# A weight-stationary product whose half block runs its 512-column products over all four banks before its 256-column ones

## The chip, the cores and the metric

The kernel runs on one core of one Trainium2 chip. The metric is the device time of one execution in microseconds (us). Five engines work side by side, each through its own queue of instructions: PE (TensorE, the matmuls; its weight loads are shown apart as PEld), DVE (VectorE), ACT (ScalarE), POOL (GpSimd) and SP (SyncE), which here only issues transfers. Matmuls write to eight banks of PSUM.

## The reference

A two-layer decoder trunk on 256 tokens of width 2048 in float32. Layer 0 mixes with eight stick-breaking attention heads and eight gated-linear-attention heads, layer 1 with a Mamba-2 state-space mixer (here "the second mixer"). After each mixer come a squared-ReLU MLP and a gated input embedding; a final RMSNorm ends it. Cut to what matters:

```python
def squared_relu_mlp(x, w_up, w_down):                 # 2048 -> 8192 -> 2048
    return jnp.square(jax.nn.relu(x @ w_up)) @ w_down

def ssd_mixer(x, w_in, ...):
    z, xbc, dt = jnp.split(x @ w_in, ...)              # 2048 -> 4096 + 6144 + 64
    ...                                                # conv, chunked scan, norm
    return (y * silu(z)) @ w_out

def reference(x, p, ...):
    h = x
    for i in range(2):
        hn = rms_norm(h, norm_mix[i])
        h = h + (sb_gla_mixer(hn, ...) if i == 0 else ssd_mixer(hn, ...))
        h = h + squared_relu_mlp(rms_norm(h, norm_mlp[i]), w_up[i], w_down[i])
        h = h + jax.nn.sigmoid(h @ ple_w_gate[i]) * (p[i] @ ple_w_proj[i])
    return rms_norm(h, final_norm)
```

Nearly all of the arithmetic lies in the products of `h` with the large weight matrices.

## The kernel before

Each operand of a large product is split in two, a rounded high part and the rest as a low part, and three of the four partial products are kept: high by high, high by low, low by high. Activations lie in memory as `[x_hi | x_lo]`, 256 columns each. Weights arrive by DMA in blocks of 1 MB (`load_block`, tile `wraw`, three buffers) and are split in half blocks of 128 x 1024 by `split_weights`: ACT casts the high part (L92, tile `whi`), DVE subtracts it for the low part (L93, tile `wlo`). Each of `whi` and `wlo` has three buffers.

`feature_major` computes the products whose output has features on partitions: the input projections of both mixers and the `up` half of each MLP. It works in groups of 512 output features, that is four PSUM banks (tiles `acc0` to `acc3`) of 128 features by 512 columns. The pool `acc_ps` holds five such banks, so that a new group finds one bank free, and gets the others when the old group's have been read. A group takes four weight blocks, each of two half blocks: eight half blocks per group. A half block holds eight stationary tiles of 128 x 128, two for each bank. With weights stationary, a bank gets from them two products of 512 columns (`whi` against `[x_hi | x_lo]`, L132) and two of 256 columns (`wlo` against `x_hi`, L137). There are 60 such groups, 480 half blocks, and 3840 products of either kind: 8 groups in the first mixer (numbers 0 to 7 in what follows), 16 in the four `up` quarters of the first MLP (8 to 23), 20 in the second mixer (24 to 43), 16 in the second MLP (44 to 59).

When a group's four banks are full they are read by the evacuation. In the MLP (`up`, L430 on) it calls `add_halves` for each bank: ACT copies the right half out (L197, tile `right`, three buffers), DVE adds the left half to it (L198). Then one DVE instruction squares (L434), and the result is split again. In the second mixer the evacuation of the `z` columns is L803 on ACT and L804 on DVE. Between its groups the second mixer also runs steps of its scan. The ones spoken of later: transposes of `xs` on PE (L721), their product with `dt` on DVE (L722, tile `xdt`), a product on POOL (L727, tile `xdd`), and a matmul of `xdd` on PE (L736, tile `st_ps`).

The other large products (`quad_major`, L371 to L373; `token_major`, L186 to L188) keep activations stationary and stream the weights; the change does not touch them.

The order in which the source issues instructions is not the order on an engine: a scheduler, with costs of its own, places the instructions of the whole program into the queues. Within a queue an instruction that waits holds up those behind it.

Of the kernel before, what the change touches and what calls it, by code (L numbers as in the profile page):

```python
# [26 lines left out]
def hybrid_trunk(  # L27
# [60 lines left out]
    def split_weights(src_raw, cols, pool=None):  # L88
        pool = pool or wts
        hi = pool.tile([P, cols], F32R, tag="whi", name="whi", padded_shape=[P, 1024])  # L90
        lo = pool.tile([P, cols], F32R, tag="wlo", name="wlo", padded_shape=[P, 1024])
        nc.scalar.copy(out=hi, in_=src_raw)  # L92
        nc.vector.tensor_tensor(out=lo, in0=src_raw, in1=hi.bitcast(F32), op=ALU.subtract)  # L93
        return hi, lo
# [3 lines left out]
    def load_block(src, cols=2048):  # L98
        raw = wts.tile([P, cols], F32, tag="wraw", name="wraw", padded_shape=[P, 2048])
        if halve.pop() if halve else False:  # L100
            nc.sync.dma_start(raw[:, : cols // 2], src[:, : cols // 2])
            nc.sync.dma_start(raw[:, cols // 2 :], src[:, cols // 2 :])
        else:
            nc.sync.dma_start(raw, src)
        return raw
# [10 lines left out]
    def feature_major(blocks, kb_n, xt, evac, width=4, kts=4, evac_group=None):  # L116

        for grp, srcs in enumerate(blocks):
            banks = [acc_ps.tile([P, 512], F32, tag="acc", name=f"acc{n}") for n in range(width)]
            cols = kts * width * P  # L120
            per = 1024 // (width * P)
            if per > kts:
                per = kts
            for kb in range(kb_n):
                raw = load_block(srcs[kb], cols)
                for c0 in range(0, kts, per):
                    hi, lo = split_weights(raw[:, c0 * width * P : (c0 + per) * width * P], per * width * P)
                    for n in range(width):
                        for j in range(per):
                            k = kb * kts + c0 + j  # L130
                            o = (j * width + n) * P
                            nc.tensor.matmul(banks[n], lhsT=hi[:, o : o + P], rhs=xt(k),  # L132
                                             start=(k == 0), stop=False, skip_group_check=True)
                        for j in range(per):
                            k = kb * kts + c0 + j
                            o = (j * width + n) * P
                            nc.tensor.matmul(banks[n][:, T : 2 * T], lhsT=lo[:, o : o + P], rhs=xt(k)[:, 0:T],  # L137
                                             start=False, stop=(k == kb_n * kts - 1), skip_group_check=True)
                yield
            if evac_group is not None:  # L140
                evac_group(grp, banks)
            else:
                for n in range(width):
                    evac(grp * width + n, banks[n])
            yield
# [274 lines left out]
    def mlp(i, x):  # L420
        r2 = []

        with tc.tile_pool(name=f"mlp{i}", bufs=2) as tmp:
# [3 lines left out]
            def up(q):  # L427
                hid[0] = operand(4, f"hid{q}_")

                def evac(grp, banks):  # L430
                    t4 = tmp.tile([P, 4, T], F32, tag="t4", name="t4")
                    for n in range(4):
                        add_halves(t4[:, n, :], banks[n])
                    nc.vector.scalar_tensor_tensor(out=t4, in0=t4, scalar=0.0, in1=t4, op0=ALU.max, op1=ALU.mult)  # L434
                    pg = hid[0](4 * grp, True)
                    nc.scalar.copy(out=pg[:, :, 0:T], in_=t4)
                    nc.vector.tensor_tensor(out=pg[:, :, T : 2 * T], in0=t4, in1=pg[:, :, 0:T].bitcast(F32), op=ALU.subtract)
                    m = 2 * grp + 1
                    if m in SEVEN:
                        a11, a21, a12, a22 = (t4[:, 2 + kk, t * P : (t + 1) * P] for kk in range(2) for t in range(2))  # L440
                        e = ev.tile([P, 4, P], F32, tag="row", name="s4")
                        nc.vector.tensor_tensor(out=e[:, 0, :], in0=a21, in1=a22, op=ALU.add)
                        nc.vector.tensor_tensor(out=e[:, 1, :], in0=e[:, 0, :], in1=a11, op=ALU.subtract)
                        nc.vector.tensor_tensor(out=e[:, 2, :], in0=a11, in1=a21, op=ALU.subtract)
                        nc.vector.tensor_tensor(out=e[:, 3, :], in0=a12, in1=e[:, 1, :], op=ALU.subtract)
                        if grp % 2 == 0:
                            sums["pg"] = page([P, 2, 1024], "ss", F32R)
                        sums[m] = sums["pg"][:, grp % 2, :]
                        ef = e.rearrange("p e t -> p (e t)")
                        nc.scalar.copy(out=sums[m][:, 0:512], in_=ef)  # L450
                        nc.vector.tensor_tensor(out=sums[m][:, 512:1024], in0=ef, in1=sums[m][:, 0:512].bitcast(F32), op=ALU.subtract)

                pace(feature_major(grid(mlp_up[i], range(4 * q, 4 * q + 4), 4), 4, x, None, evac_group=evac), [])
# [153 lines left out]
    def mixer1(xu, raw):  # L607
        with tc.tile_pool(name="mix1", bufs=1) as mid, tc.tile_pool(name="mix1t", bufs=2) as tmp:
# [159 lines left out]
            def fm(nb, evac, xt=x):  # L768
                return feature_major(grid(ssd_in, nb, 4), 4, xt, evac)
# [83 lines left out]
    def mixer0():  # L853
        with tc.tile_pool(name="mix0", bufs=1) as mid, tc.tile_pool(name="mix0t", bufs=2) as tmp:
# [52 lines left out]
            def fm(groups, evac, xt=x):  # L907
                return feature_major(grid(ab_in, groups, 4), 4, xt, evac)
# [269 lines left out]
```

## Time and profile before

| | us |
|---|---|
| median of three runs | 2729.83 (2729.3 to 2730.58) |
| the profiled execution's own time | 2729.36 |
| its span, first to last instruction | 2727.6 |
| PE busy | 2694.5 (99%) |
| DVE busy | 1908.3 (70%) |
| ACT busy | 1418.4 (52%) |
| mean granted TensorE clock | 0.997 |
| DMA, mean | 187 GB/s |

A row of a timeline is: start and duration in us, engine, line and operation, output and inputs, sizes, and how many instructions of that kind follow one another; in square brackets the idle time of the engine just before and what ended it. Matmuls are pipelined: one of 512 columns is shown with about 0.39 us, but the next starts about 0.23 us after it, so the pace is read from starts. A row of windows gives, for a stretch, its length and the busy time and number of instructions of PE, PEld, DVE, ACT and POOL, then clock, DMA share and GB/s.

### The profile page before, as it was taken

How to read it: one execution, taken by the hardware profiler on the slowest of the kernel's cores; microseconds unless marked ns; L12 is line 12 of the kernel's file. 1: busy time of each engine (PE TensorE's matmuls, PEld its weight loads, DVE VectorE, ACT ScalarE, POOL GpSimd, SP SyncE). 2: the span in 40 equal slices, each digit the busy share in tenths (PEclk: the TensorE clock that was granted, in tenths of full speed). 3: DMA queues.
4: the chain of work that ended last, by engine and by line, in shares of the span. 5: the costliest groups of instructions: out<-in, count | busy, mean ns of one | idle time of the engine just before them, and what ended most of it. 6: DMA issues, size and time to landing. Idle time of an engine off the chain costs nothing.

```text
span 2727.6 us, 35652 instructions
## 1 busy us (share of the span) xinstructions
PE 2694.5 (99%) x14004; PEld 2275.1 (83%) x14004; DVE 1908.3 (70%) x2569; ACT 1418.4 (52%) x1933; POOL 174.3 (6%) x258
## 2 busy tenths in 40 slices
PE   7999999999999999999999999999999999999998
PEld 6888878888888888888888888888888888888886
DVE  7455666776867767558988888754677776776755
ACT  6455455545545445556655655644454544545544
POOL 2000000000000000003232122300000000000000
PEclk9999999999999999999999999999999999999999
DMA  6544355555555555554555554455555555555544
GB/s 252 185 155 155 123 185 185 201 188 193 206 186 196 192 191 210 182 185 155 201 195 177 186 198 173 171 187 197 186 201 186 205 196 185 187 199 188 219 176 147
DMA packets 73304, 510.36 MB, mean 187 GB/s; under 512 B 8672, under 2 KB 8864, under 8 KB 12720
## 3 DMA queue, kind: packets, MB, share of 16 engines
q1 hardware_dynamic: 70640, 497.32, 51.3%
q10 hardware_dynamic: 2496, 10.78, 1.1%
q8 instruction: 109, 1.79, 0.3%
q14 instruction: 59, 0.48, 0.0%
HBM read 505.90 MB, written 2.16 MB: 186 GB/s over the span
## 4 chain that ended last, share of the span: by engine, by line
PE 95%; DVE 3%; ACT 1%; issue 1%; POOL 0%; DMA 0%; DVEq 0%; ACTq 0%
PE acc L132 31%; PE acc L137 15%; PE q L371 8%; PE q L373 8%; PE q L372 8%; PE acct L187 7%; PE acct L186 7%; PE acct L188 7%; DVE wlo L93 1%; PE y_ps L745 1%; PE x_tp L280 1%; PE y_ps L747 0%; DVE x L114 0%; DVE a_cv L675 0%; ACT whi L92 0%
## 5 line engine op out<-in xcount | busy, mean ns | idle before, releaser
L93 DVE TENSOR_TENSOR wlo<-wraw,whi 128x1024 fp32r<-128x1024 f32 (+1 forms) x936 | 1131.9, 1216 | 643.6 <-ACT whi L92 638.2
L92 ACT CAST whi<-wraw 128x1024 fp32r<-128x1024 f32 (+1 forms) x936 | 964.7, 1038 | 1007.5 <-PE acc L132 478.1
L132 PE MATMUL acc<-x,whi 128*128 128x512 f32 x3840 | 1213.6, 398 | 9.6 <-ACT whi L92 9.6
L137 PEld LDWEIGHTS acc<-x,wlo 128*128 128x128 f32 x3840 | 716.9, 188 | 175.7 <-DVE wlo L93 9.2
L137 PE MATMUL acc<-x,wlo 128*128 128x256 f32 x3840 | 753.4, 279 | 5.2 <-DVE wlo L93 5.1
L132 PEld LDWEIGHTS acc<-x,whi 128*128 128x128 f32 x3840 | 590.8, 189 | 19.0 <-ACT whi L92 9.8
L371 PE MATMUL q<-whi,hid 128*128 128x512 f32 x884 | 344.7, 390 | 0.0
L373 PE MATMUL q<-whi,hid 128*128 128x512 f32 x884 | 344.0, 389 | 0.0
L372 PE MATMUL q<-wlo,hid 128*128 128x512 f32 x884 | 344.0, 389 | 0.0
L373 PEld LDWEIGHTS q<-whi,hid 128*128 128x128 f32 x884 | 165.9, 188 | 34.9
L372 PEld LDWEIGHTS q<-wlo,hid 128*128 128x128 f32 x884 | 166.0, 188 | 34.2
L371 PEld LDWEIGHTS q<-whi,hid 128*128 128x128 f32 x884 | 166.0, 188 | 33.4
L186 PE MATMUL acct<-whi,x 128*128 128x512 f32 x384 | 151.1, 393 | 0.0
L188 PE MATMUL acct<-whi,x 128*128 128x512 f32 x384 | 149.7, 390 | 0.0
L187 PE MATMUL acct<-wlo,x 128*128 128x512 f32 x384 | 149.7, 390 | 0.0
L188 PE MATMUL acct<-whi,yx 128*128 128x512 f32 x256 | 100.3, 392 | 0.0
L187 PE MATMUL acct<-wlo,yx 128*128 128x512 f32 x256 | 100.2, 391 | 0.0
L186 PE MATMUL acct<-whi,yx 128*128 128x512 f32 x256 | 100.2, 391 | 0.0
L92 ACT CAST whi<-wsum 128x1024 fp32r<-128x1024 f32 x56 | 59.0, 1054 | 75.8 <-PE q L373 55.3
L93 DVE TENSOR_TENSOR wlo<-wsum,whi 128x1024 fp32r<-128x1024 f32 x56 | 68.4, 1221 | 28.6 <-ACT whi L92 28.6
L197 ACT COPY right<-acc 128x256 f32<-128x256 f32 x196 | 71.6, 369 | 30.8 <-PE acc L137 30.7
L188 PEld LDWEIGHTS acct<-whi,x 128*128 128x128 f32 x384 | 72.1, 188 | 15.1
(291 smaller groups left out, 2379.6 us busy)
## 6 DMA issues: line engine op xcount, KB each, us to landing
wraw<-in_mlp_up_dram SPq DMA_DIRECT2D x128, 1024.0 KB, 4.8
wraw<-in_mlp_down_dram SPq DMA_DIRECT2D x128, 1024.0 KB, 4.8
wraw<-in_ssd_in_dram SPq DMA_DIRECT2D x80, 1024.0 KB, 4.8
wraw<-in_ab_in_dram SPq DMA_DIRECT2D x47, 1024.0 KB, 4.8
wraw<-in_ple_gate_dram SPq DMA_DIRECT2D x32, 1024.0 KB, 4.8
wraw<-in_ssd_out_dram SPq DMA_DIRECT2D x32, 1024.0 KB, 4.7
wraw<-in_ab_out_dram SPq DMA_DIRECT2D x16, 1024.0 KB, 4.8
rb<-acs_rows ACTq DMA_DIRECT2D x8, 1024.0 KB, 4.7
```

Of the source, the lines that this page charges most:

```text
L92: nc.scalar.copy(out=hi, in_=src_raw)
L93: nc.vector.tensor_tensor(out=lo, in0=src_raw, in1=hi.bitcast(F32), op=ALU.subtract)
L132: nc.tensor.matmul(banks[n], lhsT=hi[:, o : o + P], rhs=xt(k), start=(k == 0), stop=False, skip_group_check=True)
L137: nc.tensor.matmul(banks[n][:, T : 2 * T], lhsT=lo[:, o : o + P], rhs=xt(k)[:, 0:T], start=False, stop=(k == kb_n * kts - 1), skip_group_c ...
L186: nc.tensor.matmul(banks[n], lhsT=xh, rhs=wh, start=(k == 0), stop=False, skip_group_check=True)
L187: nc.tensor.matmul(banks[n], lhsT=xh, rhs=wl, start=False, stop=False, skip_group_check=True)
L188: nc.tensor.matmul(banks[n], lhsT=xl, rhs=wh, start=False, stop=(k == kb_n * kts - 1), skip_group_check=True)
L197: nc.scalar.copy(out=right[:rows], in_=bank[:rows, T : 2 * T])
L280: nc.tensor.transpose(tp[:, j * T + t * P : j * T + t * P + P], h[:, t, (k + j) * P : (k + j + 1) * P], ident)
L371: nc.tensor.matmul(banks[b], lhsT=ah, rhs=wh, start=b not in begun, stop=False, skip_group_check=True)
L372: nc.tensor.matmul(banks[b], lhsT=ah, rhs=wl, start=False, stop=False, skip_group_check=True)
L373: nc.tensor.matmul(banks[b], lhsT=al, rhs=wh, start=False, stop=end and last[b] == m, skip_group_check=True)
```

## The change

The second inner loop gets an outer loop over the four banks of its own. A half block's eight 512-column products then stand first in the source, bank by bank, and its eight 256-column products behind them. Each bank still gets the same products with the same start and stop flags; their number and size are the same.

```diff
                     for n in range(width):
                         for j in range(per):
                             k = kb * kts + c0 + j
                             o = (j * width + n) * P
                             nc.tensor.matmul(banks[n], lhsT=hi[:, o : o + P], rhs=xt(k),
                                              start=(k == 0), stop=False, skip_group_check=True)
+                    for n in range(width):
                         for j in range(per):
                             k = kb * kts + c0 + j
                             o = (j * width + n) * P
                             nc.tensor.matmul(banks[n][:, T : 2 * T], lhsT=lo[:, o : o + P], rhs=xt(k)[:, 0:T],
                                              start=False, stop=(k == kb_n * kts - 1), skip_group_check=True)
```

Line numbers behind L133 grow by one. In 5 to 12 rows each, three places where the built programs differ.

On PE, inside a group of the first mixer, one half block over the four banks `acc_146` to `acc_149`, as a difference (`x2` is the number of products in a row):

```order
 L132 MATMUL acc_146<-x_126,whi 128x512 x2
-L137 MATMUL acc_146<-x_126,wlo 128x256 x2
 L132 MATMUL acc_147<-x_126,whi 128x512 x2
-L137 MATMUL acc_147<-x_126,wlo 128x256 x2
 L132 MATMUL acc_148<-x_126,whi 128x512 x2
-L137 MATMUL acc_148<-x_126,wlo 128x256 x2
 L132 MATMUL acc_149<-x_126,whi 128x512 x2
-L137 MATMUL acc_149<-x_126,wlo 128x256 x2
+L138 MATMUL acc_146<-x_126,wlo 128x256 x2
+L138 MATMUL acc_147<-x_126,wlo 128x256 x2
+L138 MATMUL acc_148<-x_126,wlo 128x256 x2
+L138 MATMUL acc_149<-x_126,wlo 128x256 x2
```

The four pairs of 256 columns moved behind the four pairs of 512.

On DVE, at the start of a group of the first MLP's `up`, before (`wlo_3960` and `wlo_3982` belong to the second and third half block of the new group; `acc0_3745` to `acc3_3748` are the old group's banks):

```order
L93 TENSOR_TENSOR wlo_3960<-wraw_3937,whi_3959 128x1024
L198 TENSOR_TENSOR t4_3917<-acc0_3745,right_3918 128x256
L198 TENSOR_TENSOR t4_3917<-acc1_3746,right_3921 128x256
L198 TENSOR_TENSOR t4_3917<-acc2_3747,right_3924 128x256
L93 TENSOR_TENSOR wlo_3982<-wraw_3979,whi_3981 128x1024
L198 TENSOR_TENSOR t4_3917<-acc3_3748,right_3927 128x256
L434 SCALAR_TENSOR_TENSOR t4_3917<-t4_3917 128x1024
```

and now:

```order
L93 TENSOR_TENSOR wlo_3960<-wraw_3937,whi_3959 128x1024
L93 TENSOR_TENSOR wlo_3982<-wraw_3979,whi_3981 128x1024
L199 TENSOR_TENSOR t4_3917<-acc0_3745,right_3918 128x256
L199 TENSOR_TENSOR t4_3917<-acc1_3746,right_3921 128x256
L199 TENSOR_TENSOR t4_3917<-acc2_3747,right_3924 128x256
L199 TENSOR_TENSOR t4_3917<-acc3_3748,right_3927 128x256
L435 SCALAR_TENSOR_TENSOR t4_3917<-t4_3917 128x1024
```

The subtraction for the third half block has moved ahead of the reads of the old banks. On PE the same group now begins so:

```order
L132 MATMUL acc0_3933<-x0_2888,whi_3939 128x512 x2
L138 MATMUL acc0_3933<-x0_2888,wlo_3940 128x256 x2
L132 MATMUL acc0_3933<-x0_2888,whi_3959 128x512 x2
L138 MATMUL acc0_3933<-x0_2888,wlo_3960 128x256 x2
L132 MATMUL acc0_3933<-x1_2889,whi_3981 128x512 x2
L132 MATMUL acc1_3934<-x0_2888,whi_3939 128x512 x2
L132 MATMUL acc2_3935<-x0_2888,whi_3939 128x512 x2
L132 MATMUL acc3_3936<-x0_2888,whi_3939 128x512 x2
L138 MATMUL acc1_3934<-x0_2888,wlo_3940 128x256 x2
L138 MATMUL acc2_3935<-x0_2888,wlo_3940 128x256 x2
L138 MATMUL acc3_3936<-x0_2888,wlo_3940 128x256 x2
```

The free bank, `acc0_3933`, gets the products of two and a half half blocks before `acc1_3934` gets its first; before, the first half block went over all four banks, pair of 512 and pair of 256 in turn.

On PE, at the start of group 31 in the second mixer, now:

```order
L722 MATMUL xs_tp_11904<-ident_78,xs_11632 128x128 x4
L722 MATMUL xs_tp_11910<-ident_78,xs_11632 128x128 x4
L732 MATMUL b_tp_11930<-ident_78,bc0_10200 128x128
L132 MATMUL acc0_11934<-x0_9979,whi_11940 128x512 x2
L138 MATMUL acc0_11934<-x0_9979,wlo_11941 128x256 x2
L132 MATMUL acc0_11934<-x0_9979,whi_11960 128x512 x2
L138 MATMUL acc0_11934<-x0_9979,wlo_11961 128x256 x2
L132 MATMUL acc0_11934<-x1_9980,whi_11993 128x512
L737 MATMUL st_ps_11980<-xdd_11928,b_t_11932 128x512
L132 MATMUL acc1_11935<-x0_9979,whi_11940 128x512 x2
```

The scan's matmul (`st_ps`) stands after nine of the group's products; before, it stood after the last product of the second half block, the 32nd of the group. On DVE the subtraction for `wlo_11994`, the third half block's, stands there ahead of the two products `xdt` that lead to `xdd`; before, it stood behind them.

## The prediction

> **What bounds the kernel now.** I read the page's busy times and chain first, then PE's waits, then one `up` stage by windows, then the pace of PE in timelines.
>
> ```profile
> PE 2694.5 (99%) x14004; PEld 2275.1 (83%) x14004; DVE 1908.3 (70%) x2569; ACT 1418.4 (52%) x1933; POOL 174.3 (6%) x258
> PE 95%; DVE 3%; ACT 1%; issue 1%; POOL 0%; DMA 0%; DVEq 0%; ACTq 0%
> ```
>
> PE is busy 99% of the span and 95% of the chain that ends last runs over it. Nothing else can set the time except by making PE wait.
>
> ```profile
> PE acc L132 <- ACT whi L92: 9.6, 2, 9.1
> PE acc L137 <- DVE wlo L93: 5.1, 6, 1.7
> PE dt_tp L658 <- DVE dt_work L651: 2.0, 1, 2.0
> PE r_row L256 <- DVE diag L250: 1.8, 1, 1.8
> ```
>
> These are PE's waits: line, what it waited for, us in total, times, longest. 9.1 of the first is the start of the program. For a low part PE waits 5.1 us in six places. So there is next to no idle time to win, and two things can change: PE's pace inside a half block, and new waits.
>
> ```profile
> 601.14:690.30 89.16, 89.16 (x513) 77.80 (x512) 58.28 (x71) 43.53 (x53) 0.00 (x0) 1.00 0.53 188
> 1400.00:1750.00 350.00, 349.97 (x2102) 299.07 (x2101) 283.55 (x495) 208.84 (x349) 92.34 (x117) 1.00 0.52 183
> ```
>
> The first stretch is one `up` quarter: 32 half blocks in 89.16 us, 2.786 us each, PE without a gap, DVE busy 58.28 (65%), ACT 49%. The second is most of the second mixer: DVE is busy 81%, so what comes late there comes late by DVE.
>
> **Part 1, the pace of a half block.** It has eight products of 512 columns and eight of 256.
>
> ```profile
> 999.67 0.62 PE L132 MATMUL acc<-x,whi 128*128 128x512 f32 x2
> 1000.13 0.40 PE L137 MATMUL acc<-x,wlo 128*128 128x256 f32 x2
> 1000.37 0.63 PE L132 MATMUL acc<-x,whi 128*128 128x512 f32 x2
> 1321.54 2.00 PE L132 MATMUL acc<-x,whi 128*128 128x512 f32 x8
> 1323.38 1.12 PE L137 MATMUL acc<-x,wlo 128*128 128x256 f32 x8
> 1324.33 2.01 PE L132 MATMUL acc<-x,whi 128*128 128x512 f32 x8
> 1326.18 0.60 PE L721 MATMUL xs_tp<-ident,xs 128*128 128x128 f32 x4
> ```
>
> The first three rows are the old order: 0.46 us for two of 512, 0.24 for two of 256, 0.70 together, four times that for a half block. The last four rows are from the second mixer, where the scheduler had put a half block into the new order already: eight of 512 in 1.84 us (1323.38 − 1321.54), eight of 256 in 0.95 (1324.33 − 1323.38), 2.79 together. So the order in which the change puts the products costs 2.79 where the old one costs 2.786: 0.004 × 480 half blocks = +1.9, I take **+2**.
>
> Bounds: the fastest pace of 512-column products is that of a long run of them.
>
> ```profile
> 1119.93 0.39 PE L373 MATMUL q<-whi,hid 128*128 128x512 f32 x1
> ...
> 1122.65 0.39 PE L373 MATMUL q<-whi,hid 128*128 128x512 f32 x1
> ```
>
> Twelve in 2.72 us, 0.2267 each. With eight at this pace and 0.95 for the rest a half block takes 2.764, 0.022 less: −10.6. At the other end the second row of eight (1324.33 to 1326.18) took 1.85; with 0.95 that is 2.80, 0.014 more: +6.7. I take the middle of what was measured for this very sequence.
>
> [...]
>
> **Part 2, starts of groups in the MLP.** There the order changes more than the diff says. A new group finds one free bank; the others come when the old group's are read. Before, three of the four reads on DVE stood ahead of the third half block's subtraction; now that subtraction stands ahead of all four, and PE fills the first bank with two and a half half blocks, then asks for the second. By the orders this is so at 26 of 60 starts: 3 in each of the eight `up` quarters, 2 in the first mixer. The rows for the sum are from one such start, whose first product begins at 1015.00 (call it T0):
>
> ```profile
> 1013.80 0.37 ACT L197 COPY right<-acc 128x256 f32<-128x256 f32 x1 [0.30 <-PE acc L137]
> 1014.30 0.63 PE L132 MATMUL acc<-x,whi 128*128 128x512 f32 x2
> 1014.40 1.07 DVE L198 TENSOR_TENSOR t<-acc,right 128x256 f32<-128x256 f32 x3
> 1014.97 1.05 ACT L92 CAST whi<-wraw 128x1024 fp32r<-128x1024 f32 x1
> 1015.00 0.62 PE L132 MATMUL acc<-x,whi 128*128 128x512 f32 x2
> 1016.05 1.23 DVE L93 TENSOR_TENSOR wlo<-wraw,whi 128x1024 fp32r<-128x1024 f32 x1 [0.57 <-ACT whi L92]
> 1017.19 0.42 DVE L198 TENSOR_TENSOR t<-acc,right 128x256 f32<-128x256 f32 x1
> ```
>
> The cast starts 0.05 after the last use of its buffer (1014.30 + 0.63 = 1014.93 to 1014.97), the subtraction 0.03 after the cast (1016.02 to 1016.05), and the next DVE instruction 1.14 after that (1016.05 to 1017.19), with 0.42 for one read. With the new order:
> - the old group's last product of 512 columns starts 0.95 + 0.23 = 1.18 before T0 and ends at −0.79; the cast runs from −0.74 to +0.31;
> - the subtraction starts at +0.34 (the buffer that it writes is free when the old group's last product ends, about +0.16), the read of the first bank at +1.48, done at +1.90;
> - ACT's copies follow the cast, the first by +0.7; they are not last;
> - PE needs the bank after 3 × 0.46 + 2 × 0.24 = 1.86.
>
> So PE waits, with 0.05 from DVE's end to the load, until 1.95: 0.09. After a wait a load stands open:
>
> ```profile
> 56.25 1.76 DVE L93 TENSOR_TENSOR wlo<-wraw,whi 128x1024 fp32r<-128x1024 f32 x1
> 58.06 0.30 PEld L137 LDWEIGHTS acc<-x,wlo 128*128 128x128 f32 x2 [1.60 <-DVE wlo L93]
> 58.07 0.38 PE L137 MATMUL acc<-x,wlo 128*128 128x256 f32 x1 [1.17 <-DVE wlo L93]
> ```
>
> DVE's end (58.01) to the load is the 0.05; two loads take 0.30, so one shows some 0.1 beyond the first: I take 0.1 for it. 0.2 × 26 = **+5.2**. Bounds: nothing where one of the steps is 0.1 shorter; 0.5 each, 13, where the cast or a copy is held up by another 0.3, as the copy at 1013.80 was. The later banks follow at DVE's 0.36 a read (1.07 for three), under PE's 0.46 for a pair.
>
> [...] In the rows the last read, at 1017.19, indeed begins only when the subtraction lets it.
>
> **Part 3, starts in the second mixer.** At six groups (31, 33, 37, 39, 41, 43) the scan's matmul `st_ps` is moved forward, to between the ninth and tenth product of the group. Its input goes over DVE (`xdt`) and POOL (`xdd`), and `xdt` now stands behind the third subtraction.
>
> ```profile
> 1409.85 1.04 PE L721 MATMUL xs_tp<-ident,xs 128*128 128x128 f32 x8
> 1410.64 1.28 DVE L722 TENSOR_TENSOR xdt<-xs_tp,dt_t 128x512 f32<-128x512 f32 x2
> 1410.75 0.71 PE L132 MATMUL acc<-x,whi 128*128 128x512 f32 x2
> 1411.57 1.05 POOL L727 TENSOR_TENSOR xdd<-xdt,dec 128x512 f32<-128x512 f32 x1
> 1416.42 1.02 PE L736 MATMUL st_ps<-xdd,b_t 128*128 128x512 f32 x2
> ```
>
> In the old order `st_ps` came 5.67 after T0 (1410.75), 3.80 after `xdd` was done. In the new one: the transposes take 0.90 ahead of T0, so the cast runs from −1.64 to −0.59, the subtraction from −0.56 to +0.58, the first `xdt` (0.68 in the group's mean, half of 1.28 here) to 1.26, `xdd` with its 1.05 to 2.40 with a handover of 0.1, the load at 2.45. PE is there at 4 × 0.35 + 0.23 = 1.63. Wait 0.82, and 0.1 for the load: 0.9 × 6 = **+5.4**. Bounds: 0.5 each (3) where DVE's queue is ahead, 1.8 (11) where another DVE instruction of 1.2 stands in front, as the 81% of the stage allow. No other group start shows such a step moved forward; I cost those 28 at nothing, since a `quad_major` product, or scan work of PE's own, gives DVE its time there.
>
> **Part 4, the gain.** In steady groups the low part is needed 1.84 into a half block, not 0.46, so a late subtraction hurts less. All such waits are 5.1 us; in the stretch with 1.17 of them DVE has no gap (from 40 to 66 us it is busy 26.00 of 26.00), and then lateness only moves on.
>
> ```profile
> 40.00:66.00 26.00, 23.72 (x133) 19.73 (x132) 26.00 (x36) 17.18 (x29) 12.45 (x13) 1.00 0.49 170
> ```
>
> I take **−1**, bounds 0 and −5. Transfers are no part of it: the number and order of the weight blocks stays, and the DMA share is 0.53 in the `up` stage.
>
> **Sum.** +2 + 5.2 + 5.4 − 1 = +11.6 on the profiled execution's own 2729.36: 2741.0. The median of the runs is 0.47 above that execution, so 2741.4; I predict **2741**, slower by 0.4%.
>
> **Rivals.**
> - *The runs of like products recover the pace of the long stream* (the other side). At 0.2267 for 512 columns a half block takes 2.764 and the steady part gives −10.6; the group starts' loads hide, or cost half of 10.6, and the time is 2729.8 − 10.6 + 5.3 − 1 = 2723.5. It decides from a half block below 2.77. For it: the pace of `quad_major`. Against: the sequence itself, in the trace, twice at 2.79 and 2.80. Chance 0.08.
> - *The waits at the starts don't come*: the margin of part 2 is 0.09 us, and part 3 leans on DVE being no earlier than I let it be. Then +2 − 1 is left: 2731. For it: the scheduler moved these instructions by costs of its own, under which they fit. Against: it puts the subtraction in front of four reads that PE asks for. Chance 0.27.
> - *DVE's load makes more starts late*: the other 14 starts of the second mixer lose 0.9 each as well: +12.6, 2754. For it: DVE at 81%. Against: `st_ps` isn't moved there. Chance 0.13.
> - That the change doesn't do what it says: the orders show it does, but for the group starts, which are part of the sum.
>
> My forecast has the rest, 0.52. **How the numbers follow.** Range 2728 to 2752: from the second rival with its own spread of 3 to the forecast with the upper bounds of one of its large terms; left out are the first rival and most of the third, 0.2. No change is within 0.2%, 5.5 us, about what a measurement of this kernel can tell: 2724.4 to 2735.3. The forecast falls in it where both terms come out at half, 0.07; with the second rival, 0.34. Faster 0.08, slower 0.58.
>
> **What would show it.** Part 1: a half block inside `up` at 2.79 to 2.80 by starts, rows of x8; wrong if below 2.78. Part 2: in PE's waits a line for L132 on DVE's reads (L199), 26 times of 0.1 to 0.3, and an `up` quarter of 89.3 plus 3 × 0.2. Part 3: `st_ps` waiting on POOL some 0.8, six times. Part 4: fewer than six waits of L138 on `wlo`. The prediction is wrong if the page shows no such waits and the same pace, or if the starts' waits are near a microsecond each.

## The result, and the profile after

The changed kernel takes 2755.06 us (median of four runs, 2751.93 to 2755.57) where the kernel before takes 2729.57 in the same comparison: a ratio of 1.009 (95% interval 1.0078 to 1.0102). It is slower, as forecast, but by 25 us where the prediction had 11.6, and it lies outside the range of 2728 to 2752. The profiled execution took 2751.93, its span is 2750.2; against the profile before (2727.6) that is 22.6 more.

The page's busy times and chain, after:

```profile
PE 2706.2 (98%) x14004; PEld 2285.2 (83%) x14004; DVE 1907.7 (69%) x2569; ACT 1407.9 (51%) x1933; POOL 152.4 (6%) x258
PE 94%; DVE 3%; ACT 2%; issue 0%; POOL 0%; DMA 0%; DVEq 0%; ACTq 0%; POOLq 0%
```

TensorE still bounds it. It has the same 14004 instructions and is shown busy 11.7 us longer, so half of the loss isn't shown as idle time at all: it is work at a slower clock (mean granted clock 0.996, before 0.997) and at a slightly slower pace, and short waits of weight loads, which the view doesn't show as idle PE (see the MLP below). The other half stands in TensorE's waits (line, what it waited for, us in total, times, longest):

```profile
PE acc L132 <- ACT whi L92: 10.5, 3, 9.2
PE acct L188 <- DVE wlo L93: 7.8, 2, 7.0
PE acc L138 <- DVE wlo L93: 6.2, 5, 5.0
PE st_ps L737 <- POOL xdd L728: 3.0, 5, 0.7
PE acct L187 <- ACT whi L92: 1.2, 1, 1.2
```

The fourth row is the forecast wait of the scan's matmul (the view puts the sixth, 0.7, down to DVE's L805). The second is in no term of the sum: one wait of 7.0 us at L188, in `token_major`, which the change doesn't touch.

To place the loss I took the time at which each group's first product starts, before and after:

| from | to | before, us | added, us |
|---|---|---|---|
| start | group 3 | 0 to 86 | −2.35 |
| group 3 | group 7 | 86 to 300 | −0.49 |
| group 7, first mixer's out projection | group 8 | 300 to 427 | +9.50 |
| group 8 (first MLP) | group 24 | 427 to 1228 | +3.40 |
| group 24 (second mixer) | group 27 | 1228 to 1306 | +2.59 |
| group 27 | group 44 | 1306 to 1916 | +6.52 |
| group 44 (second MLP) | end | 1916 to 2728 | +3.40 |

They add up to 22.57. Four of these places can be read off directly.

**The MLP**, by windows (length, busy time of PE, PEld, DVE, ACT, POOL, clock, DMA share, GB/s), the same `up` quarter as before, and the start of group 23 in the timelines of PE and DVE:

```profile
608.63:698.65 90.02, 90.02 (x513) 78.33 (x512) 57.49 (x69) 42.32 (x51) 0.00 (x0) 1.00 0.54 189
```

```profile
1022.05 2.00 PE L132 MATMUL acc<-x,whi 128*128 128x512 f32 x8
1023.89 1.11 PE L138 MATMUL acc<-x,wlo 128*128 128x256 f32 x8
1024.84 0.63 PE L132 MATMUL acc<-x,whi 128*128 128x512 f32 x2
...
1026.24 2.21 PE L132 MATMUL acc<-x,whi 128*128 128x512 f32 x8
```

```profile
1025.17 1.23 DVE L93 TENSOR_TENSOR wlo<-wraw,whi 128x1024 fp32r<-128x1024 f32 x1 [1.57 <-ACT whi L92]
1026.32 1.41 DVE L199 TENSOR_TENSOR t<-acc,right 128x256 f32<-128x256 f32 x4
```

The half block takes 1024.84 − 1022.05 = 2.79. With T0 = 1024.84 the subtraction starts at +0.33 and the first read at +1.48; the prediction had +0.34 and +1.48. Who waited for these reads in the first MLP (the view of L199, total us and times):

```profile
  PEld acc L132: 4.2, 12
```

The weight loads wait at 12 starts, 0.35 each. The loads of these rows start 0.11 to 0.23 ahead of their products (1024.73 for the product at 1024.84, 1025.08 for that at 1025.31), so PE itself loses less, and no wait of PE is shown for it, only the row of eight that takes 2.21 instead of 2.00: 0.21. The quarter is 0.86 longer.

**The scan's matmul** at group 31, the timelines of DVE, POOL and PE:

```profile
1424.18 1.28 DVE L723 TENSOR_TENSOR xdt<-xs_tp,dt_t 128x512 f32<-128x512 f32 x2
```

```profile
1424.95 1.04 POOL L728 TENSOR_TENSOR xdd<-xdt,dec 128x512 f32<-128x512 f32 x1 [9.46 <-DVE xdt L723]
```

```profile
1423.61 0.71 PE L132 MATMUL acc<-x,whi 128*128 128x512 f32 x2
...
1426.05 1.13 PE L737 MATMUL st_ps<-xdd,b_t 128*128 128x512 f32 x2 [0.56 <-POOL xdd L728]
```

`xdd` ends 2.38 after T0 (1423.61), forecast 2.40; the matmul starts at 2.44, forecast 2.45. The six waits are 0.56 to 0.66 each. Groups 31, 33, 37, 39 and 41 are 0.85 to 0.96 longer than before.

**The out projection of the first mixer**, timelines of ACT, DVE and PE:

```profile
341.33 2.93 ACT L92 CAST whi<-wraw 128x1024 fp32r<-128x1024 f32 x3
```

```profile
344.97 1.67 DVE L1072 SCALAR_TENSOR_TENSOR og<-og,gn,norm 128x256 f32<-128x256 f32 x4
346.55 1.09 DVE L1099 TENSOR_TENSOR og<-og,gg 128x256 f32<-128x256 f32 x3
347.56 1.09 DVE L111 TENSOR_TENSOR o_gla<-og,o_gla 128x256 fp32r<-128x256 f32 x3
...
348.90 1.22 DVE L93 TENSOR_TENSOR wlo<-wraw,whi 128x1024 fp32r<-128x1024 f32 x1
```

```profile
342.42 0.73 PE L187 MATMUL acct<-whi,o_sb 128*128 128x512 f32 x2 [1.17 <-ACT whi L92]
350.17 0.80 PE L188 MATMUL acct<-wlo,o_sb 128*128 128x512 f32 x1 [7.02 <-DVE wlo L93]
```

The high part is cast by 342.4. The low part of the same weights starts at 348.90, because VectorE's queue now has the scaling, the gating and the splits of the GLA heads' output ahead of it. TensorE runs nothing in the 7.02 us, though the next product in its queue (L189) needs only the high part, which L187 had at 342.42. Before, DVE ran in that place:

```profile
345.58 1.22 DVE L93 TENSOR_TENSOR wlo<-wraw,whi 128x1024 fp32r<-128x1024 f32 x1
346.72 1.22 DVE L219 SCALAR_TENSOR_TENSOR norm<-norm 128x1024 f32<-128x1024 f32 x1
347.97 1.23 DVE L220 SCALAR_TENSOR_TENSOR norm<-norm 128x1024 f32<-128x1024 f32 x1
349.11 1.22 DVE L93 TENSOR_TENSOR wlo<-wraw,whi 128x1024 fp32r<-128x1024 f32 x1
```

with low parts in between. And the wait leaves something behind. The windows after it (us, PE busy, clock, DMA share, GB/s):

```profile
346.00:348.00 2.00, 0.00 (x0) 0.63 0.00 0
348.00:350.00 2.00, 0.00 (x0) 0.50 0.00 0
350.00:352.00 2.00, 1.83 (x4) 0.50 0.53 78
352.00:354.00 2.00, 2.00 (x7) 0.66 0.95 397
```

The granted clock falls to half some 3.4 us into the wait and stays there until about 353.4, so the 3.2 us of work after 350.17 are done at half speed, 1.6 lost: products of 512 columns start 0.43 apart there (350.77 to 351.19 and on) and 0.23 apart after 353.6. Wait 7.02 + 1.17, clock 1.6, less the 1.50 that TensorE waited there for `o_gla` before: 8.3 of the 9.50. Another 0.9 is only moved: four small products of the GLA heads now stand behind group 7's first product, so group 6 is 0.9 shorter and this stretch longer. (The run below of all groups but 7, which hasn't the long wait, still has 0.91 less there and 0.89 more here.)

**Group 26 of the second mixer**, timelines of ACT, DVE and PE, and the windows behind the wait:

```profile
1293.84 1.03 ACT L92 CAST whi<-wraw 128x1024 fp32r<-128x1024 f32 x1
1299.54 1.74 DVE L642 RECIPROCAL dt_work<-dt_work 64x256 f32<-64x256 f32 x1
1301.84 1.21 DVE L93 TENSOR_TENSOR wlo<-wraw,whi 128x1024 fp32r<-128x1024 f32 x1
1303.11 2.08 PE L138 MATMUL acc<-x,wlo 128*128 128x256 f32 x8 [5.04 <-DVE wlo L93]
```

```profile
1304.00:1306.00 2.00, 2.00 (x9) 0.50 0.87 283
1306.00:1308.00 2.00, 2.00 (x7) 0.50 0.58 242
```

Here too a subtraction stands behind other work of VectorE, 7 us after the cast of its high part. But the idle time is nearly the same as before: TensorE waited 4.8 us in groups 24 to 26 then, in four pieces of at most 1.96 and at full clock, and 5.04 now in one. What is new is the clock: it is at half for 6.8 us from 1302.3, 6.0 of them with work, which loses 3.0, more than the whole 2.59 of the stretch. In the second profile of the changed kernel the wait is the same, 3.4 us are at half clock, and the stretch adds 1.40.

### The profile page after: what moved, and what is told of

Read it like the earlier page. It is cut to its first block, busy times and chain, and to the rows that moved or that the text cites. A ratio compares the mean times of both kernels' runs of the same rounds, so it can differ in the third digit from the quotient of the medians.

```text
span 2750.2 us, 35649 instructions
## 1 busy us (share of the span) xinstructions
PE 2706.2 (98%) x14004; PEld 2285.2 (83%) x14004; DVE 1907.7 (69%) x2569; ACT 1407.9 (51%) x1933; POOL 152.4 (6%) x258
## 4 chain that ended last, share of the span: by engine, by line
PE 94%; DVE 3%; ACT 2%; issue 0%; POOL 0%; DMA 0%; DVEq 0%; ACTq 0%; POOLq 0%
PE acc L132 31%; PE acc L138 15%; PE q L372 8%; PE q L373 8%; PE q L374 8%; PE acct L188 6%; PE acct L189 6%; PE acct L187 6%; DVE wlo L93 1%; PE x_tp L281 1%; PE y_ps L746 1%; ACT whi L92 1%; PE y_ps L748 0%; DVE yx L114 0%; PE st_ps L737 0%
## 5 line engine op out<-in xcount | busy, mean ns | idle before, releaser
L132 PE MATMUL acc<-x,whi 128*128 128x512 f32 x3840 | 997.1, 397 | 11.0 <-ACT whi L92 10.5
L132 PEld LDWEIGHTS acc<-x,whi 128*128 128x128 f32 x3840 | 684.3, 189 | 142.2 <-ACT whi L92 10.9
L138 PEld LDWEIGHTS acc<-x,wlo 128*128 128x128 f32 x3840 | 535.5, 190 | 54.0 <-DVE wlo L93 8.6
L138 PE MATMUL acc<-x,wlo 128*128 128x256 f32 x3840 | 551.0, 283 | 6.2 <-DVE wlo L93 6.2
L187 PE MATMUL acct<-whi,x 128*128 128x512 f32 x384 | 151.0, 393 | 0.0
L188 PE MATMUL acct<-wlo,x 128*128 128x512 f32 x384 | 149.7, 390 | 0.0
L189 PE MATMUL acct<-whi,x 128*128 128x512 f32 x384 | 149.7, 390 | 0.0
L188 PE MATMUL acct<-wlo,yx 128*128 128x512 f32 x256 | 99.8, 390 | 0.8 <-DVE wlo L93 0.8
L189 PE MATMUL acct<-whi,yx 128*128 128x512 f32 x256 | 100.2, 391 | 0.0
L187 PE MATMUL acct<-whi,yx 128*128 128x512 f32 x256 | 100.1, 391 | 0.0
L189 PEld LDWEIGHTS acct<-whi,x 128*128 128x128 f32 x384 | 72.1, 188 | 15.1
L187 PEld LDWEIGHTS acct<-whi,x 128*128 128x128 f32 x384 | 72.1, 188 | 14.6
```

Source lines behind the costliest of these rows:

```text
L187: nc.tensor.matmul(banks[n], lhsT=xh, rhs=wh, start=(k == 0), stop=False, skip_group_check=True)
L188: nc.tensor.matmul(banks[n], lhsT=xh, rhs=wl, start=False, stop=False, skip_group_check=True)
L189: nc.tensor.matmul(banks[n], lhsT=xl, rhs=wh, start=False, stop=(k == kb_n * kts - 1), skip_group_check=True)
```

## The experiments

All kernels below are the changed one with a condition `late` for a half block's order (`no` the group, 0 to 59, `hb` the half block in it, 0 to 7), unless said otherwise:

```diff
-                    for n in range(width):            # 512-column products
-                        ...
-                    for n in range(width):            # 256-column products
-                        ...
+                    for part in (((0,), (1,)) if late else ((0, 1),)):
+                        for n in range(width):
+                            for low in part:
+                                ...
```

### One group alone, and all but that one

My theory for the largest piece was that the scheduler's order on VectorE in the out projection hangs on group 7, the one just ahead of it.

```diff
+                    late = no == 7
```

> The old order in all groups but number 7, the last of the first mixer's input projection: 8 of 480 half blocks have the new order. Theory (the out projection of the first mixer waits because the scheduler now puts the norm and gate work of the GLA heads on VectorE ahead of the low parts of the out weights): the same 7 us wait of L188's kind on the low part appears and the time is 2730 + 9.5 = 2739, with everything else as before. Rival (the loss of group 7's stretch belongs to many groups, or to late weights): 8 half blocks cost 8 x 0.006 and the time is 2730.

```diff
+                    late = no != 7
```

> The new order in all groups but number 7. Theory: VectorE's queue in the out projection is the old one, the 7 us wait is gone, 2755 - 9.5 = 2745.5. Rival (the wait comes with any of the earlier groups' shift in time): it stays, 2755.

Group 7 alone: 2738.54, a ratio of 1.0034 (1.0021 to 1.0047) to 2729.96. All but group 7: 2744.4, 1.0054 (1.0039 to 1.0069). Both as the theory has it. In the first, eight of 480 half blocks cost 8.6 us. TensorE's waits are those of the kernel before, without the 1.5 for `o_gla` and with

```profile
PE acct L194 <- DVE wlo L93: 7.0, 1, 7.0
PE acct L193 <- ACT whi L92: 1.2, 1, 1.2
```

(L194 is L188 with six lines more, L193 is L187.) Group 8 starts 8.7 later than group 7 did, each against the kernel before, and the next 18 groups add nothing. Group 27 adds 1.1: the clock is at half there for 3.4 us, with the same waits as in the kernel before, where it isn't.

### The cause of the 7 us wait, taken away

That the wait is VectorE's queue was so far read from the timeline. This run issues the last norm and gate work of the heads behind the first steps of the out projection; all the work is done.

```diff
+            def rms_gla(m):           # newton and scaling, for heads 4 to 7 called from gla_tail
+                ...
-            for hh in range(8):
-                nc.vector.tensor_tensor(out=og[:, hh, :], in0=og[:, hh, :], in1=gg[:, hh, :], op=ALU.mult)
-                split_into(o_x(8 + hh), og[:, hh, :])
-            return out_stage(ab_out, 4, o_x, 2)
+            def gla_tail():
+                for hh in range(8):
+                    if hh == 4:
+                        rms_gla(1)
+                    ...               # the same two lines
+                    if hh % 4 == 3:
+                        yield
+            return out_stage(ab_out, 4, o_x, 2, first=gla_tail())
```

> The changed kernel, with the last norm and gate work of the GLA heads issued in the source behind the first steps of the out projection; on VectorE two low parts of the out weights then stand 7 and 9 instructions earlier, ahead of the scaling and gating of the heads. Theory (the 7 us wait is VectorE's queue): the first low part comes at most 3 us after its cast instead of 7.6, so the wait falls by about 5 and with it the half clock behind it (1.6); a wait for o_gla of 1.5 as in the kernel before may come back: 2755 - 6 = 2749, 2747 to 2751. Rival (the wait is for weights or for TensorE's own order): 2754 to 2755.

> The same edit on the kernel before. VectorE's low parts stand there where they stood, within one place. Theory: no change, 2728 to 2731. Rival (the edit is worth something by itself, the 1.5 us for o_gla): 2728.

On the changed kernel: 2748.45 (1.0068, 1.0051 to 1.0085), where it had 1.009 and, in another run, 1.0086 without the edit: 5 to 6 us less. The stretch from group 7 to group 8 is 4.6 longer than before instead of 9.5. On the kernel before: 2730.48 against 2730.41 (1.0001, 0.9991 to 1.001), nothing. DVE and PE of the first:

```profile
344.65 1.22 DVE L93 TENSOR_TENSOR wlo<-wraw,whi 128x1024 fp32r<-128x1024 f32 x1
345.79 1.22 DVE L220 SCALAR_TENSOR_TENSOR norm<-norm 128x1024 f32<-128x1024 f32 x1
346.92 1.22 DVE L93 TENSOR_TENSOR wlo<-wraw,whi 128x1024 fp32r<-128x1024 f32 x1
```

```profile
344.38 0.73 PE L187 MATMUL acct<-whi,o_sb 128*128 128x512 f32 x2 [1.17 <-ACT whi L92]
345.93 0.51 PE L188 MATMUL acct<-wlo,o_sb 128*128 128x512 f32 x1 [0.81 <-DVE wlo L93]
```

With the low part moved ahead the wait is 0.81 instead of 7.02. So it is VectorE's queue. The 1.5 us for `o_gla` did not come back, and the half clock did not go away altogether (last section).

### The last half block, and all the others

At the starts of groups, is it the first half block's order that costs, or the old group's last? The two runs split the change between them.

```diff
+                    late = hb < 7
```

> The new order in half blocks 1 to 7 of each group, the old one in the last. Theory (starts lose time because the old group's four banks all finish within the last 0.95 us of it): with the old order in the last half block bank 0 is finished about 2.1 us before the end again, the waits at the 26 starts (0.25 each by the trace) and of st_ps at the six (0.9 each) are gone, and the out projection has its old VectorE order. What is left is the pace, 420 half blocks by 0.006 = 2.5, and the gain at the program's start, up to -4.6: 2726 to 2733. Rival (starts lose time by the first half block's order, whose banks 1 to 3 are asked for 0.23 us earlier each): at least 0.2 at 26 starts, 2735 or more.

```diff
+                    late = hb == 7
```

> The new order in the last half block of each group alone, 60 of 480; the complement of the run that kept the old order there. Theory (the loss comes with the last half block, whose four banks finish together): the scheduler moves the third subtraction ahead of the reads and st_ps forward as in the changed kernel, so 27 starts by 0.2 = 5.4, 7 by 0.9 = 6.3 and the out projection's 9.4 are lost, with next to nothing for the pace (60 x 0.008 = 0.5): 2730 + 21.6 = 2751. Rival (the loss belongs to the half blocks in proportion): an eighth of 25, 2733.

New order in seven half blocks of eight: 2731.85, 1.0009 (0.9999 to 1.0019). New order in the last alone: 2754.03, 1.0085 (1.0069 to 1.0102). The 60 last half blocks carry nearly the whole loss, and the other 420 cost 2 us together, with an interval that reaches nothing. So it isn't the order in which a new group begins that costs, but the old group's last half block. That comes with two things at once, four banks that finish together and the scheduler's new order on VectorE, and no run has one without the other. Without them TensorE has no wait for `st_ps` and no load waits for a read of the MLP; with them alone all of these are there:

```profile
PE acct L194 <- DVE wlo L93: 9.5, 2, 7.0
PE acc L141 <- DVE wlo L93: 6.6, 6, 3.5
PE st_ps L743 <- POOL xdd L734: 4.0, 7, 0.7
```

The two runs also give both sizes apart. In the first, group 8 starts 1.54 ahead of the kernel before and group 24 only 0.66: 0.88 lost in 16 groups of seven new half blocks, 0.008 for each. In the second, each start inside the first MLP's quarters adds 0.20 (groups 9 to 11: 9.86, 10.05, 10.25, 10.47 behind from one start to the next).

The second run came 3 us above its forecast. Its profile has a second wait of `acct` for a low part, 2.5 us at the second mixer's out projection where the changed kernel has 0.8, and half clock behind it; from group 43 to 44 it adds 4.2 where the changed kernel adds 0.9. Why the scheduler's order falls out worse there than with the whole change is open.

### By stages

```diff
+                    late = 24 <= no < 44
```

> The new order in the 20 groups of the second mixer alone. Theory: the sum by stages holds, 9.1 us there by the changed kernel's trace (six starts by 0.9 = 5.4, the rest the 5 us wait in group 26 and the pace): 2739. Rival (the waits depend on where the earlier stages left VectorE): the second mixer alone loses half or less, 2734 or below.

```diff
+                    late = 8 <= no < 24 or no >= 44
```

> The new order in the 32 groups of the two MLPs alone. Theory: 24 starts by 0.2 and 32 groups by 0.06 for the pace, 4.8 + 2.0 = 6.8: 2736.8. Rival (in a stage where VectorE is busy 65% the starts hide): 2730 + 2.0 = 2732.

Second mixer alone: 2738.17 (1.003, 1.0018 to 1.0041), 8.4 lost where the trace of the whole change had 9.1. MLPs alone: 2737.06 (1.0025, 1.0015 to 1.0034), 7.3 against 6.8. Both are near the sum by stages, and both rivals lie outside the intervals, which reach some 3 us to either side. So the losses belong to their stages in the main. The second mixer's run has the wait of 5.0 us in group 26 again, so that one too comes from the order in its own stage.

### The first two groups

```diff
+                    late = no < 2
```

> The new order in groups 0 and 1 alone, the first 50 us, where VectorE has no gap. Theory (a low part that is needed 1.84 us into a half block instead of 0.46 hides lateness there): the 4.6 us that the changed kernel is ahead by the start of group 2 are kept in part, since group 2 gave 2.2 back: 2725 to 2728. Rival (lateness only moves on, VectorE's work is the bound there): 2730.

2730.04 against 2729.96 (0.9998, 0.9988 to 1.0007): the rival. Group 2 starts 1.92 early and group 3 0.21 late, so what was gained is given back at once: VectorE has no gap there (before, it is busy 26.00 of 26.00 us from 40 to 66 us), and a low part that may come later only moves the lateness on. The whole change gives the same back in group 2 (4.56 early at its start, 2.35 at the next); what it kept is taken up under part 4.

### The changed kernel once more

> The changed kernel once more, for the spread of its runs and a second profile. Theory (its first profile shows no half clock after the gap at 28 us, where the kernel before shows 3 us of it, and its times are 2751.9 once and 2754.8 to 2755.6 three times at a mean clock lower by 0.001): runs fall into two groups some 3 us apart, and a profile of the slower group shows the half clock in one more place. Rival (the spread is evenly distributed and the clock is the same in both): no such place.

2754.01 (1.0086, 1.0071 to 1.0101). The four runs are 2752.56 and 2752.85 with a mean clock of 0.996, 2755.16 and 2755.26 with 0.995: two groups, with the clock. The profile is of the upper clock again and has, like the first, no half clock near 30 us. So which place the other group has at half clock is not shown.

## Why the prediction was wrong

**Part 1, the pace: right in mechanism, mis-sized.** The term was 0.004 per half block, +2. The run without the last half blocks shows 0.008, which is 3.8 for 480. The rows it was taken from are rounded to 0.01.

**Part 2, starts in the MLP: right.** +5.2 was forecast as 26 × 0.2; measured 0.20 per start. That the old group's last half block brings it is shown by the pair of runs; how much is the banks that finish together and how much the reads behind the subtraction isn't told apart. The sign to look for was wrong in one point: the wait stands with the loads (L132 on L199, 12 times in the first MLP), and PE itself shows one alone, 0.5 in the first mixer.

**Part 3, starts in the second mixer: right for the six, wrong for the rest.** Of +5.4 the profile shows 5.46 with the pace in it. The step that failed is that new waits were priced at the starts of groups alone and everything else was put at nothing; its last sentence gives as the reason that a `quad_major` product or the scan's own work gives VectorE its time. The two large losses lie at no start. The wait of 7.02 stands in the out projection behind group 7, whose stretch adds 9.50; the wait of 5.04 begins 10 us behind the start of group 26, and groups 24 to 26 add 2.59. In both a subtraction stands behind other work in VectorE's queue, 6.5 and 7.0 us after the cast of its high part. For the first wait the run with the mended queue shows that this is the cause; for the second the runs show only that it comes with the order in its own stage, and the queue is read from the timeline. In the out projection the scheduler had reordered VectorE's queue in a stage whose own source, and whose order on TensorE, hardly changed. Nor had the sum a term for the clock behind a long wait, which loses 1.6 behind the first and 3.0 behind the second.

**Part 4, the gain: the sign right by luck.** Taken as −1, shown −2.35 by group 3. The run of the first two groups says that lateness only moves on, as the part's own caution had it. TensorE's waits of L138 for a low part are five instead of six, but 6.2 us, since the 5.0 of group 26 is among them. Two other things make up more than the 2.35. 1.7 is the clock around 32 us: before, there are 3.4 us at half clock after the gap at 28 us, and after the change there are none. Another 1.1 is the first half block, where products run at about half their later pace for a while (before, a pair of 512 columns takes 0.86, 10.98 to 11.84, and 0.46 in the next half block, 14.43 to 14.89): it takes 5.30 us before (9.13 to 14.43) and 4.20 after (9.19 to 13.39), but 5.13 in the run of the first two groups, whose order there is the same. That run also has the 3.4 us at half clock, and nothing of the gain is left in it. (The clock is at half near 30 us in all six profiles with the old order at the start, and in one of six with the new one.)

```profile
30.00:32.00 2.00, 1.24 (x5) 0.75 0.00 0
32.00:34.00 2.00, 2.00 (x6) 0.50 0.01 4
34.00:36.00 2.00, 2.00 (x13) 0.89 0.51 127
```

These are the windows before: 2 × (0.25 + 0.50 + 0.11) = 1.72 us of clock missing.

**The rivals.** *DVE's load makes more starts late* gave the time best, 2754, but by luck, since its mechanism is another: 14 starts at 0.9. The groups 30, 32, 34, 38, 40 and 42 of the second mixer are 0.03 to 0.06 longer, which is their pace, and 35 and 36 are 0.3. That the waits at the starts don't come is out, since each start shows its 0.20 or 0.9. That TensorE's runs recover the pace is out: no run shows a half block below 2.78 in a whole quarter. So the terms that the sum had come to 3.8 + 5.2 + 5.1 (six starts without their pace) − 3.6 (what the first seven groups gained, −2.8, without the 0.8 that pace and two starts cost there) = 10.5. That this is near the forecast's 11.6 is in part luck, since the 3.6 is no gain of part 4's kind but the 2.8 just named and the 0.9 that is only moved. The other 12.1 of the 22.6 are in the two stretches without a term, 9.5 and 2.6.

No version beats the kernel before. With the new order in all but the last half blocks it is 0.09% slower, with an interval that reaches no change; with it in the first two groups alone it is the same.

## What to carry to other kernels

Where a scheduler orders a whole program, an edit in one loop can reorder a feeder engine's queue in a stage that doesn't contain the loop: compare the queues of every engine that TensorE waits for over the whole program, above all where one stage hands over to the next, before a term is set to nothing. When several accumulators are to be read and reused, look at the work that finishes them: here, finishing all four together in the last half block brought nearly the whole loss (2754.03), and finishing them one after another in that half block took it away (2731.85). And price a wait of several microseconds on TensorE at more than its length, since the clock was at half behind the two here (1.6 and 3.0 us of work lost); before, four shorter waits of nearly the same sum in groups 24 to 26, 4.8 us, left it at 1.00.

## What the runs showed of the hardware that I had not expected

Where TensorE still had work ahead, the granted clock went to half for 3.4 us or for twice or three times that. By windows of 2 us, the time at half clock is 3.4 us before (at 30 to 35 us), 6.8 after the change at 346 to 353 and again after the 5.0 us wait in group 26, and 3.4 in the run with the mended queue, where TensorE had waited 1.17 and 0.81 just ahead. In the second profile of the changed kernel the same two waits of 7.0 and 5.0 us brought 10.2 and 3.4. The run with the mended queue:

```profile
346.00:348.00 2.00, 2.00 (x6) 0.66 0.57 111
348.00:350.00 2.00, 2.00 (x6) 0.50 0.98 414
```

A piece of 3.4 us that falls on work costs half of it, 1.7. And only short waits stood ahead of some pieces: the 1.17 and 0.81 us here, and 1.77 and 0.46 in the kernel before, at its start:

```profile
30.30 0.71 PE L256 MATMUL r_row<-diag,ones 128*128 128x128 f32 x4 [1.77 <-DVE diag L250]
31.47 2.93 PE L132 MATMUL acc<-x,whi 128*128 128x512 f32 x6 [0.46 <-ACT whi L92]
```

Six products of 512 columns begin 0.455 us apart there (31.47 to 34.20), where it is 0.23 at full clock. In the run of the first two groups the waits ahead of the half clock were shorter still, 1.04 and 0.46. Its order of instructions at the start is that of the five profiles in which the clock near 30 us is whole, so the order alone doesn't decide it. What does is not shown.
